# Channel shuffle on one core: tiles of 32 KB a partition in place of 24 KB, three buffers a side in place of four

## Chip, cores, metric

One core of a Trainium2 chip. The time is the device time of one execution in microseconds (us). A run of a kernel gives one such time; each kernel was run several times, and medians are quoted with lowest and highest. The profile is one recorded execution; its span, from the first to the last instruction, is about 1.8 us shorter than the time of the same execution. The TensorE clock granted was 1.0 of full speed in every run. A run more than 1.5% above the fastest of its kernel is called slow and left out of the comparisons; the others are called fast.

## The reference

```python
x = x.reshape(batch, h, w, groups, channels_per_group)   # 16, 64, 64, 8, 32, float32
x = x.transpose(0, 1, 2, 4, 3)
return x.reshape(batch, h, w, c)                         # 16, 64, 64, 256
```

No arithmetic: in each pixel's 256 channels an 8 x 32 table is transposed. 67.11 MB are read and 67.11 MB written.

## The kernel before

A tile takes 128 x q consecutive pixels. Each of the 128 partitions gets q pixels, which are q x 256 floats or q KB, one contiguous run in HBM, the memory outside the core; the distance between the starts of two partitions' runs, here also q KB, is called the row pitch. The load is issued from SP, the copy that permutes runs on VectorE (DVE in the profile), the store is issued from ACT. A tile pool of n buffers means that load i+n waits for copy i, and copy i+n for store i.

```python
_SIZES = [4, 8, 16] + [24] * 20 + [4]
_IN_BUFS = 4
_OUT_BUFS = 4
# ... pools in_pool and out_pool with these numbers of buffers, each of the biggest size
    for q in _SIZES:
        in_tile = in_pool.tile([P, biggest * c], F32, name="in_tile")
        nc.sync.dma_start(out=in_tile[:, : q * c], in_=rows(x_flat, first, q))
        out_tile = out_pool.tile([P, biggest * c], F32, name="out_tile")
        nc.vector.tensor_copy(
            out=out_tile[:, : q * c].rearrange("p (i j g) -> p i j g", j=CPG, g=G),
            in_=in_tile[:, : q * c].rearrange("p (i g j) -> p i j g", g=G, j=CPG),
        )
        nc.scalar.dma_start(out=rows(out_flat, first, q), in_=out_tile[:, : q * c])
        first += P * q
```

## Time and profile before

| | before |
|---|---|
| time | 317.05 us (316.96 to 317.16, 3 runs) |
| span of the profile | 315.3 us |
| VectorE busy | 122.0 us, 39% |
| moved | 134.22 MB, 426 GB/s over the span, 432 in the middle |
| load, issue to landing (median) | 52.3 us |
| store, issue to landing (median) | 31.2 us |

Most views of this profile are in the prediction. One more, the groups of instructions with shapes kept apart, is what the copies' costs were taken from. After the count come busy time in us and mean ns of one copy, then the idle time before these copies and what ended it.

```profile
L49 DVE COPY out_tile<-in_tile 128x6144 f32<-128x6144 f32 x20 | 113.9, 5694 | 169.2 <-DMA in_tile<-in_x_dram 169.2
L49 DVE COPY out_tile<-in_tile 128x4096 f32<-128x4096 f32 x1 | 3.9, 3881 | 3.9 <-DMA in_tile<-in_x_dram 3.9
L49 DVE COPY out_tile<-in_tile 128x2048 f32<-128x2048 f32 x1 | 2.0, 2024 | 1.4 <-DMA in_tile<-in_x_dram 1.4
```

VectorE idles longer than it works, and always until a load lands.

### The profile page before, as it was taken

How to read it: one execution, taken by the hardware profiler on the slowest of the kernel's cores; microseconds unless marked ns; L12 is line 12 of the kernel's file. 1: busy time of each engine (PE TensorE's matmuls, PEld its weight loads, DVE VectorE, ACT ScalarE, POOL GpSimd, SP SyncE). 2: the span in 40 equal slices, each digit the busy share in tenths (PEclk: the TensorE clock that was granted, in tenths of full speed). 3: DMA queues.
4: the chain of work that ended last, by engine and by line, in shares of the span. 5: the costliest groups of instructions: out<-in, count | busy, mean ns of one | idle time of the engine just before them, and what ended most of it. 6: DMA issues, size and time to landing. Idle time of an engine off the chain costs nothing.

```text
span 315.3 us, 178 instructions
## 1 busy us (share of the span) xinstructions
DVE 122.0 (39%) x24; POOL 0.2 (0%) x4
## 2 busy tenths in 40 slices
DVE  2525706243351707071533426170706244351710
POOL 0000000000000000000000000000000000000000
DMA  8999999999999999999999999999999999999997
GB/s 318 409 398 438 431 433 446 421 430 446 424 427 446 424 427 446 424 427 446 424 427 446 427 424 446 430 421 446 433 418 446 433 418 446 436 418 446 419 443 319
DMA packets 6912, 134.22 MB, mean 426 GB/s; under 512 B 768, under 2 KB 768, under 8 KB 1280
## 3 DMA queue, kind: packets, MB, share of 16 engines
q1 hardware_dynamic: 3456, 67.11, 49.9%
q10 hardware_dynamic: 3456, 67.11, 49.5%
HBM read 67.11 MB, written 67.11 MB: 426 GB/s over the span
## 4 chain that ended last, share of the span: by engine, by line
DMA 36%; another core or an unknown queue 33%; DVE 26%; SPq 0%; issue 0%; DVEq 0%
DMA in_tile<-in_x_dram 36%; DVE out_tile L49 26%; SPq L47 0%; DVEq L49 0%
## 5 line engine op out<-in xcount | busy, mean ns | idle before, releaser
L49 DVE COPY out_tile<-in_tile 128x6144 f32<-128x6144 f32 (+3 forms) x24 | 122.0, 5082 | 181.6 <-DMA in_tile<-in_x_dram 181.6
L71 POOL MEMSET const-bfloat16-1.0<- 128x1 bf16 x1 | 0.1, 101 | 0.0
L71 POOL MEMSET const-uint8-127<- 128x1 uint8 x1 | 0.1, 101 | 0.0
L71 POOL MEMSET const-float32-0.0<- 128x1 f32 x1 | 0.1, 98 | 0.2 <-issue 0.2
L71 POOL MEMSET const-float32-1.0<- 128x1 f32 x1 | 0.1, 98 | 0.0
## 6 DMA issues: line engine op xcount, KB each, us to landing
in_tile<-in_x_dram SPq DMA_DIRECT2D x20, 3072.0 KB, 52.3
out_dram<-out_tile ACTq DMA_DIRECT2D x20, 3072.0 KB, 31.2
in_tile<-in_x_dram SPq DMA_DIRECT2D x1, 2048.0 KB, 11.0
out_dram<-out_tile ACTq DMA_DIRECT2D x1, 2048.0 KB, 23.5
in_tile<-in_x_dram SPq DMA_DIRECT2D x2, 512.0 KB, 24.8
in_tile<-in_x_dram SPq DMA_DIRECT2D x1, 1024.0 KB, 5.5
out_dram<-out_tile ACTq DMA_DIRECT2D x2, 512.0 KB, 11.7
out_dram<-out_tile ACTq DMA_DIRECT2D x1, 1024.0 KB, 19.0
```

Of the source, the lines that this page charges most:

```text
L49: nc.vector.tensor_copy(out=out_tile[:, : q * c].rearrange("p (i j g) -> p i j g", j=CPG, g=G), in_=in_tile[:, : q * c].rearrange("p (i g ...
L71: nc = _bacc.Bacc("TRN2", target_bir_lowering=False, num_devices=1)
```

## The change

Its intent: fewer and larger transfers in the same memory. Per partition, 2 x 4 buffers of 24 KB and 2 x 3 buffers of 32 KB are both 192 KB. The small tiles at the ends stay.

```diff
-_SIZES = [4, 8, 16] + [24] * 20 + [4]
-_IN_BUFS = 4
-_OUT_BUFS = 4
+_SIZES = [4, 8, 16] + [32] * 15 + [4]
+_IN_BUFS = 3
+_OUT_BUFS = 3
```

## The prediction

> **What bounds the kernel now.** The kernel only moves data: every tile is loaded, its channels are permuted by one VectorE copy, and it is stored. I read the page first, for the engines and the totals:
>
> ```profile
> span 315.3 us, 178 instructions
> DVE 122.0 (39%) x24; POOL 0.2 (0%) x4
> DMA  8999999999999999999999999999999999999997
> GB/s 318 409 398 438 431 433 446 421 430 446 424 427 446 424 427 446 424 427 446 424 427 446 427 424 446 430 421 446 433 418 446 433 418 446 436 418 446 419 443 319
> DMA packets 6912, 134.22 MB, mean 426 GB/s; under 512 B 768, under 2 KB 768, under 8 KB 1280
> ```
>
> VectorE works 39% of the span. The DMA engines are full in every slice but the first and the last, and the rate repeats round 432 GB/s with no dip. The 134.22 MB are the input read once and the output written once, which the change cannot reduce. The packet line tells how tiles become packets: 24 tiles x 2 directions x (128 partition rows + 16 small ones) = 6912, and the small ones, 24 x 2 x 16 = 768, are those under 512 B. So one partition's row of a tile is one packet, of 24 KB now; I take the 16 small ones to be completion marks.
>
> Next the windows, cut at the starts of copies, to separate the steady stretch from the ends:
>
> ```profile
> 2.00:6.66 4.66, 1.10 (x2) 0.00 (x0) 1.00 1.02 412
> 6.66:12.61 5.95, 2.02 (x2) 0.00 (x0) 1.00 1.01 399
> 12.61:22.09 9.48, 3.88 (x2) 0.00 (x0) 1.00 1.01 418
> ...
> 46.66:293.90 247.24, 96.83 (x17) 0.00 (x0) 1.00 1.00 432
> 293.90:302.40 8.50, 5.68 (x1) 0.00 (x0) 1.00 1.02 438
> 302.40:313.30 10.90, 1.10 (x1) 0.00 (x0) 1.00 0.98 419
> ```
>
> The columns end with DMA share and GB/s. From 46.66 to 293.90 us seventeen copies start, one every 247.24 / 17 = 14.543 us. In that time a 24 KB tile goes in and another out: 2 x 128 x 24576 B = 6.291 MB, which makes 432.6 GB/s. At that rate all 134.22 MB would take 310.3 us; the span is 315.3. The other 5.0 us are the ends: 2.0 us before data flows, about 1.0 us because the stretch from 2.00 to 22.09 us moves 8.26 MB where 432.6 GB/s needs 19.1 us of its 20.1, and some 2 us at the end, while the last stores drain and the completions come back. The measured 317.05 us are 1.75 us more than the span.
>
> Last the waits, for what keeps the queues fed:
>
> ```profile
> DVE out_tile L49 <- DMA in_tile<-in_x_dram: 181.6, 24, 8.9
> SPq L47 <- DVE out_tile L49: 105.1, 20, 5.8
> in_tile<-in_x_dram SPq DMA_DIRECT2D x20, 3072.0 KB, 52.3
> out_dram<-out_tile ACTq DMA_DIRECT2D x20, 3072.0 KB, 31.2
> ```
>
> All 24 copies wait for their load, none for a store buffer. A load is issued when the copy four tiles earlier ends and lands when its own copy begins: 4 x 14.54 - 5.7 = 52.5 us, and the listing says 52.3. So three loads or more are always queued. A store lands 31.2 us after issue, two tile times. Both queues always hold work: the transfer rate is the bound, and VectorE's regular 8.8 us of idling is its consequence.
>
> **What the Trainium skill says.** (1) "DMA: Bandwidth & Descriptors", section "Where 436 GB/s comes from", puts a ceiling of 435.2 GB/s on the DMA side of SBUF. The trace agrees: 432.6 is 99.4% of it, leaving hardly anything for larger packets to win. (2) The same page, "Anatomy of one DMA — SWDGE (gpsimd) path", gives each DMA a fixed cost of about 2 us, mostly the wait for the last byte's receipt. These transfers are issued from SP and ACT, not that path, and the trace shows the cost hidden: two such DMAs end in each 14.543 us, while the bytes alone need 6.291 MB / 435.2 GB/s = 14.456 us. Only 0.087 us a tile is left for all overhead. (3) The same page, "Latency and other measured facts", has copies slowing when HBM row pitches are large powers of two: 207 GB/s a direction at 512 KiB against 214 at full rate, 164 at 2 MiB. Our pitch becomes 32 KiB, sixteen times below the first of these. The trace has one 16 KB-pitch tile and its rate says little, as it mixes with small stores. (4) "Perfetto Trace Analysis", "Identifying Performance Opportunities", reads repeated bubbles on the engine that should be saturated as a possible lack of buffers. The bubbles here are on VectorE, which should not be saturated; the DMA engines have none.
>
> **The change part by part.** *Bytes and buffers.* 28 + 20 x 24 + 4 = 512 KB a partition becomes 28 + 15 x 32 + 4 = 512. Buffers stay at 4 x 24 + 4 x 24 = 3 x 32 + 3 x 32 = 192 KB a partition. The byte time of 310.3 us stays.
>
> *Fewer transfers.* Twenty large loads and stores become fifteen; packets become 19 x 2 x 144 = 5472 if a 32 KB row stays one packet. If the 0.087 us a tile is all paid per packet or per DMA, five tiles fewer save 5 x 0.087 = 0.43 us; if it is proportional to bytes, nothing. I take 0.25 us. The new tile time is then between 14.543 x 4/3 = 19.39 and 14.456 x 4/3 + 0.087 = 19.36 us.
>
> *Copies.* By shape the listing gives 2024, 3881 and 5694 ns for 2048, 4096 and 6144 elements, so the last 2048 cost 1.81 us and a copy of 8192 takes about 7.5 us. Busy: 15 x 7.5 + 2 x 1.10 + 2.02 + 3.88 = 120.6 us (was 122.0). It lies beside the transfers, with 19.4 - 7.5 = 11.9 us idle before each. Worth 0.
>
> *Three load buffers.* Load i+3 is issued when copy i ends. Load i+1 has by then run 7.5 of its 19.4 us and i+2 is queued behind it, so the load queue holds (19.4 - 7.5) + 19.4 = 31 us of work at each refill. Landing time 3 x 19.4 - 7.5 = 50.6 us, near the old 52.3. At the start the first 32 KB load must now wait for copy 0, which ends at 5.25 us; the loads ahead of it are busy until 12.6 us. Worth 0.
>
> *Three store buffers.* This is the tighter place. Now a store is done 5.7 + 31.2 = 36.9 us after its tile landed, 2.54 tile times, where 4 = 58.2 us are allowed: 21 us spare. The lag arises at the start, where small store packets alternate with large load packets, so I expect it to keep its size counted in tiles. Then after the change a store is done 2.54 x 19.4 = 49.2 us after its tile landed, landing about 42 us after issue, where 3 x 19.4 = 58.2 us are allowed: 9 us spare. Worth 0. Even if a copy had to wait, the load queue's 31 us would have to run dry first.
>
> *The ends.* The opening 4, 8, 16 and the closing 4 KB tile are the same, so the 5.0 us stay. When the last large tile lands, its store comes 7.5 us later (was 5.7). The stores still queued then are 1.5 tiles (2.54 less the tile just landed), 30 us of work at half the rate or 15 us alone, so no hole opens.
>
> Sum: 317.05 - 0.25 + 0 + 0 + 0 = 316.8 us.
>
> **The rivals.** *A fixed cost per DMA that really is paid.* At the skill's 2 us, five transfers fewer in each queue, with the queues side by side, would save 10 us: 307 us, 3% faster. For it: the smaller tiles of the first 22 us do run slower. Against it: the 0.087 us above; a saving of 10 us would require about 447 GB/s over the steady part, above the ceiling, and the trace holds no slice-long average over 446. *Power-of-two rows.* Rows 32 KB apart may make engines that march together meet in one part of HBM. At the 3% that the skill gives for 512 KiB (207 against 214) on the 290 us of large tiles: 9 us more, 326 us. For it: 24 KB rows are no power of two, so before cannot show it. Against: the skill's smallest slow pitch is far larger, and here tiles lie contiguously. *Store buffers run out.* If the store lag exceeds three tiles, copies begin to wait for stores, VectorE's idle time is split between the two, and loads are issued later. With 31 us of loads queued I would give that 0 to 2 us: up to 319 us. For it: spare time falls from 21 to 9 us. Against: the lag in before is steady, with all large stores near the median of 31.2 (maximum 31.3).
>
> **Range and chances.** The sum of known effects spans 316.6 to 317.05. Widened by small losses at the ends and a milder form of the pitch or buffer rival, 315.8 to 318.4 should hold eight times in ten. Over 2% faster (under 310.7) needs the ceiling broken: 0.01. Over 2% slower (over 323.4) needs the pitch rival nearly whole: 0.04. Within 2%: 0.95.
>
> **What would show it.** Right: large copies 19.36 to 19.39 us apart, each about 7.5 us and waiting only for its load; some 432 to 434 GB/s in the middle slices; 5472 packets; loads landing in about 50.6 us, stores in about 42; the first and last slices as before. Wrong: a middle rate under 428 (pitch), copies that wait for stores (buffers), tile times clearly under 19.3 us (a per-DMA cost), more packets than 5472 (rows split), or a hole in the last 20 us.

## The result and the profile after

After: 316.84 us (316.67 to 316.93, 4 runs). Before, beside it: 317.06 us (316.96 to 317.16, 4 runs). The ratio is 0.9995, 95% interval 0.998 to 1.001: the same. (Here and below a ratio is the mean time of one kernel's fast runs over that of the other's of the same rounds, so not quite the ratio of the medians quoted.)

The head of the page after, with the lines that answer to those of before:

```profile
span 315.2 us, 150 instructions
...
DVE 119.9 (38%) x19; POOL 0.2 (0%) x4
...
DMA  8999999999999999999999999999999999999996
GB/s 314 408 422 458 403 449 408 457 408 453 412 453 412 458 412 453 420 445 428 437 428 437 437 428 437 428 437 433 437 433 437 428 441 424 445 420 426 439 441 291
DMA packets 5472, 134.22 MB, mean 426 GB/s; under 512 B 608, under 2 KB 608, under 8 KB 1120
```

The span, the mean rate and the full row of nines are those of before. The rate swings more from slice to slice in the first half (403 to 458), which no run explains; from 80 to 280 us both kernels move 433 GB/s. There are 5472 packets, as worked out: a 32 KB row is still one packet.

The copies by shape, then the two waits and the landing times of the large transfers:

```profile
L49 DVE COPY out_tile<-in_tile 128x8192 f32<-128x8192 f32 x15 | 111.9, 7459 | 166.2 <-DMA in_tile<-in_x_dram 166.2
```

```profile
DVE out_tile L49 <- DMA in_tile<-in_x_dram: 179.3, 19, 11.9
SPq L47 <- DVE out_tile L49: 105.1, 16, 7.6
```

```profile
in_tile<-in_x_dram SPq DMA_DIRECT2D x15, 4096.0 KB, 50.5
out_dram<-out_tile ACTq DMA_DIRECT2D x15, 4096.0 KB, 42.4
```

All 19 copies wait for their load and none for a store, as before. The load's landing time of 50.5 us is 3 x 19.37 - 7.5 = 50.6: a load is issued the moment a copy frees its buffer, and two more are queued ahead of it.

The windows after, cut at the starts of copies, with DMA share and GB/s last:

```profile
2.00:6.66 4.66, 1.11 (x1) 0.00 (x0) 1.00 1.03 417
6.66:12.74 6.08, 2.02 (x2) 0.00 (x0) 1.00 1.05 412
12.74:24.38 11.64, 3.83 (x2) 0.00 (x0) 1.00 1.02 432
...
74.22:287.23 213.01, 82.03 (x11) 0.00 (x0) 1.00 1.00 433
287.23:298.20 10.97, 7.47 (x2) 0.00 (x0) 1.00 1.01 435
298.20:313.20 15.00, 1.08 (x1) 0.00 (x0) 1.00 0.97 415
```

From 74.22 to 287.23 us eleven copies start, one every 213.01 / 11 = 19.365 us. With the 14.543 us of before this gives the two terms of a tile: 8.389 - 6.291 = 2.097 MB more take 19.365 - 14.543 = 4.822 us, so bytes go at 434.9 GB/s, and 14.543 - 6.291 MB / 434.9 GB/s = 0.077 us a tile is left for everything else. Twenty large tiles cost 20 x 14.543 = 290.9 us and fifteen 15 x 19.365 = 290.5. The steady part gave 0.4 us by this sum. The medians differ by 0.2 us, so the ends should have taken the other 0.2 back; but the interval above includes no difference at all, so neither figure is shown by the times.

### The profile page after: what moved, and what is told of

Same layout as the page of the kernel before. It is cut to its first block, busy times and chain, and to the rows that moved or that the text cites. A ratio compares the mean times of both kernels' runs of the same rounds, so it can differ in the third digit from the quotient of the medians.

```text
span 315.2 us, 150 instructions
## 1 busy us (share of the span) xinstructions
DVE 119.9 (38%) x19; POOL 0.2 (0%) x4
## 2 busy tenths in 40 slices
DMA packets 5472, 134.22 MB, mean 426 GB/s; under 512 B 608, under 2 KB 608, under 8 KB 1120
## 4 chain that ended last, share of the span: by engine, by line
DMA 40%; another core or an unknown queue 30%; DVE 25%; issue 0%; DVEq 0%; SPq 0%
DMA in_tile<-in_x_dram 40%; DVE out_tile L49 25%; DVEq L49 0%; SPq L47 0%
## 5 line engine op out<-in xcount | busy, mean ns | idle before, releaser
L49 DVE COPY out_tile<-in_tile 128x8192 f32<-128x8192 f32 (+3 forms) x19 | 119.9, 6313 | 179.3 <-DMA in_tile<-in_x_dram 179.3
## 6 DMA issues: line engine op xcount, KB each, us to landing
in_tile<-in_x_dram SPq DMA_DIRECT2D x15, 4096.0 KB, 50.5
out_dram<-out_tile ACTq DMA_DIRECT2D x15, 4096.0 KB, 42.4
in_tile<-in_x_dram SPq DMA_DIRECT2D x1, 2048.0 KB, 11.1
```

The costliest lines, as they stand in the source:

```text
L49: nc.vector.tensor_copy(out=out_tile[:, : q * c].rearrange("p (i j g) -> p i j g", j=CPG, g=G), in_=in_tile[:, : q * c].rearrange("p (i g ...
```

## The experiments

Theory: the transfer rate is the bound, tile size and buffers are spare, and a tile costs its bytes at 434.9 GB/s plus about 0.08 us. Rivals: three buffers hurt and large tiles hid it; large tiles gain and the power-of-two row pitch takes it back; a fixed cost per transfer is really paid; VectorE or the small tiles at the ends are on the path. All kernels gave the correct result. They came in three batches, on different chips, each beside its own runs of the kernel before: 316.94, 316.96 and 316.99 us. The ratios below are to these. The kernel after was not run again beside them.

### Three buffers, old tiles

```diff
-_SIZES = [4, 8, 16] + [32] * 15 + [4]
+_SIZES = [4, 8, 16] + [24] * 20 + [4]    # 3 load and 3 store buffers kept
```

> Half of the change alone: 24 KB tiles as before, but three load and three store buffers. Theory (the transfer rate binds, buffers are spare): 317.0 us, within 0.3 of the kernel before; tiles 14.54 us apart; loads landing in about 3 x 14.54 - 5.7 = 37.9 us, stores in 31.2, no copy waiting for a store (done 36.9 us after the tile landed, 43.6 allowed). Rival (three buffers are too few and the change's larger tiles hid that): 319 us or more, with copies that wait for stores.

Measured: 317.00 us (316.91 to 317.03), ratio 1.0001 (0.9988 to 1.0013). Loads landed in 37.8 us, stores in 30.5, all 24 copies waited for loads. The fourth pair of buffers was worth nothing; three buffers of either size are enough.

### Rows of 30 KB

```diff
-_SIZES = [4, 8, 16] + [32] * 15 + [4]
+_SIZES = [4, 8, 16] + [30] * 16 + [4]
```

> Sixteen tiles of 30 KB, a row pitch that is no power of two, with three buffers each. Theory (a tile costs its bytes at 434.9 GB/s plus 0.077 us, from the tile times 14.543 and 19.365 us of the two kernels): tiles 7.864 MB / 434.9 GB/s + 0.077 = 18.16 us apart, 316.8 to 316.9 us in all. Rival (a gain from fewer transfers was given back to the power-of-two pitch of 32 KB): tiles clearly under 18.1 us apart and under 315.5 us in all.

Measured: 316.52 us (316.50 to 316.63), ratio 0.9987 (0.9975 to 1.000). Copies 70.92 to 288.81 us are 217.89 / 12 = 18.16 us apart, the theory's figure. So no gain was hidden behind the 32 KB pitch. The time is 0.3 us below the forecast, at the ends since the middle is as forecast, and is the lowest of all kernels here, but its interval reaches 1.

### Tiles of 8 KB

```diff
-_SIZES = [4, 8, 16] + [32] * 15 + [4]
-_IN_BUFS = 3
-_OUT_BUFS = 3
+_SIZES = [4] + [8] * 63 + [4]
+_IN_BUFS = 12
+_OUT_BUFS = 12
```

> 63 tiles of 8 KB between two of 4, with twelve buffers each, so the same memory. It takes the cost per tile times 65 in place of 19. Theory (0.077 us a tile): tiles 2.097 MB / 434.9 GB/s + 0.077 = 4.90 us apart, and 46 x 0.077 = 3.5 us more than after in all, about 320 us. Rival (about 2 us per transfer really paid, in each queue): 46 x 2 = 92 us more, about 409 us. A cost of 0.5 us would show as 340 us.

Measured: 321.47 us (321.45 to 322.05), ratio 1.0148 (1.0132 to 1.0164). That is 4.6 us more than after for 46 more tiles, 0.10 us a tile where 0.077 were expected. The fixed cost is real, but for a load and a store together it is a twentieth of 2 us. This is with further transfers always queued; no run has the cost without them. Whether it is paid by the DMA or by its packets is not separated, as each tile has the same number of both.

### Two buffers a side

```diff
-_IN_BUFS = 3
-_OUT_BUFS = 3
+_IN_BUFS = 2
+_OUT_BUFS = 2
```

> The kernel after with two load and two store buffers. A store needs 49.2 us from the landing of its tile and only 2 x 19.37 = 38.7 are now allowed, so copies must wait for stores. Theory (a copy's wait costs only if both DMA queues run dry, and at any moment a store is queued): 317 to 318.5 us, the waits of the copies now split between loads and stores. Rival (waits for store buffers are paid in full): 10 us at each of some 13 tiles, over 400 us; paid in part: over 323 us.

Measured: 318.24 us (317.90 to 319.11), ratio 1.0044 (1.0031 to 1.0058). The list of waits turned over, while the middle kept its rate:

```profile
DVE out_tile L49 <- DMA out_dram<-out_tile: 180.6, 17, 12.3
DVE out_tile L49 <- DMA in_tile<-in_x_dram: 5.3, 2, 3.9
```

```profile
62.00:280.00 218.00, 87.44 (x12) 0.00 (x0) 1.00 1.00 433
```

Seventeen copies now wait for a store buffer, 180.6 us in all, and it costs 1.3 us against the kernel before, outside the middle. The lesson is in these two fences together: VectorE's waits changed their releaser, and the rate in the middle did not change. I had expected the waits to be split between loads and stores. They are all put down to the stores, because a load and the store before it now finish almost together and the store is last.

### Each copy twice

```diff
-        nc.vector.tensor_copy(...)
+        for _ in range(2):
+            nc.vector.tensor_copy(...)       # the same copy
```

> The kernel after with every copy done twice (same result). VectorE works 240 of 317 us. Theory (copies lie beside transfers): a store is done 49.2 + 7.5 = 56.7 us after its tile landed at most, 58.1 allowed; 316.8 to 317.4 us, large copies in pairs of 15 us, tiles still 19.37 us apart. Rival (the copy is on the path, by its end or by the issue of loads): 15 x 7.5 = 112 us more if in full, 7.5 us more (324) if only the last copy is exposed.

Measured: 317.13 us (316.94 to 318.71, 6 runs), ratio 1.0016 (1.0001 to 1.0031); five of the six lie within 316.94 to 317.90. VectorE worked 241.8 us of a 316.6 us span in the profiled run, the one at 318.71. In that run tiles were 19.50 us apart, not the 19.37 expected; the runs nearer the median have no profile. 120 us of added work cost about 0.2 us in the median: the copy is beside the transfers.

### The last tile a large one

```diff
-_SIZES = [4, 8, 16] + [32] * 15 + [4]
+_SIZES = [4, 8, 16, 4] + [32] * 15
```

> The kernel after with the closing 4 KB tile moved to the start, so that the last tile is one of 32 KB. Theory (30 us of stores at half rate, or 15 us alone, are queued when the last tile lands, so its copy of 7.5 us is covered): 316.6 to 317.2 us. Rival (the small last tile shortens the exit): the exit grows by 7.5 - 1.1 = 6.4 us, 323 us.

Measured: 316.91 us (316.81 to 316.96), ratio 0.9998 (0.9986 to 1.001). The last copy, of 7.5 us, is covered by stores still queued. The small closing tile is worth nothing.

### No small tiles

```diff
-_SIZES = [4, 8, 16] + [32] * 15 + [4]
+_SIZES = [32] * 16
```

> Sixteen equal tiles of 32 KB, no small tile at either end, three buffers each. Theory (time is bytes over rate plus about 2 us at each end; a full queue of loads keeps the engines busy until stores come): the rate is 433 GB/s from about 2 us on, the 1.0 us that small tiles cost at the start is won back, 315.6 to 316.2 us; store lag only about two tile times, as large rows now alternate with large ones from the start. At the end the store of the last tile comes 7.5 us after its landing and the stores queued then last about as long, so up to 1 us may be lost. Rival (the small tiles fill the pipeline early and that is worth what they bring forward): the first store starts 14 us later than in the kernel after and the time is up to 14 us longer, 325 to 331 us.

Measured: 324.30 us (323.67 to 324.92), ratio 1.0231 (1.0218 to 1.0245): 2.3% slower, where my theory expected a small gain. The rival named about the right size, but for a reason that the profile refutes: it put the loss into a late start. The time is lost in the middle. Here is the timeline of this kernel's copies (start, duration, shape, idle before and its releaser):

```profile
41.33 7.50 DVE L49 COPY out_tile<-in_tile 128x8192 f32<-128x8192 f32 x1 [11.26 <-DMA in_tile<-in_x_dram]
61.36 7.50 DVE L49 COPY out_tile<-in_tile 128x8192 f32<-128x8192 f32 x1 [12.52 <-DMA in_tile<-in_x_dram]
81.51 7.61 DVE L49 COPY out_tile<-in_tile 128x8192 f32<-128x8192 f32 x1 [12.65 <-DMA in_tile<-in_x_dram]
...
300.64 7.57 DVE L49 COPY out_tile<-in_tile 128x8192 f32<-128x8192 f32 x1 [11.88 <-DMA in_tile<-in_x_dram]
```

Copies are (300.64 - 61.36) / 12 = 19.94 us apart, 3% more than the 19.365 of the kernel after, with the same tiles, buffers and waits. The stretch from 80 to 280 us moved 424 GB/s, where the kernel after moved 433 (columns as in the windows above; then the stores' landing time):

```profile
80.00:280.00 200.00, 75.36 (x10) 0.00 (x0) 1.00 1.00 424
out_dram<-out_tile ACTq DMA_DIRECT2D x16, 4096.0 KB, 34.4
```

The trace's packet records say which packets: from 80 to 280 us a 32 KB load packet took 1259 ns in the mean and the slowest hundredth over 1950, a store packet 1215; in the kernel after both take 1213. So the loads are what slows, and only some of them: 13.9% of the load packets took over 5% longer than usual, and none in the kernel after.

### No small tiles at the start only

```diff
-_SIZES = [4, 8, 16] + [32] * 15 + [4]
+_SIZES = [32] * 15 + [24, 8]
```

> Fifteen tiles of 32 KB, then 24 and 8; no ramp at the start. Theory: as sixteen equal tiles, but the last store is asked for 2 us after its landing instead of 7.5, so no hole can open at the end: 315.4 to 316.0 us, the fastest so far by about 0.3%. Rival (early small tiles matter): 325 to 331 us.

Measured: 324.09 us (323.70 to 324.61), ratio 1.0228. The same loss and again 424 GB/s in the middle, so the end is not its place. What the missing small tiles do to the middle, 40 us and more after they would have been done, was open. One clue is the offset between the two streams. With sixteen equal tiles the first store is issued at 20.4 us, two us before the second load has landed (its copy starts at 22.6), so the first store and the third load set out almost together, and from then on a store follows a load through the tiles at a short distance. The last batch varied that.

### A first tile of 4 KB

```diff
-_SIZES = [32] * 16
+_SIZES = [4, 28] + [32] * 15
```

> Sixteen equal tiles were 7 us slower, against the theory, and their middle ran at 424 GB/s in place of 433. Here the first of them is split in 4 and 28, so all later tiles have the same addresses as there. Theory P (the middle is slow because stores walk through their rows nearly in step with the loads, a store finishing 2 to 4 us after a load; a small first tile starts stores while the next load is under way and sets another offset): the middle is back at 433 GB/s, tiles 19.37 us apart, 316.0 to 316.8 us. Theory A (the 4 MB alignment of the addresses slows the middle): 323 to 325 us.

Measured: 317.04 us (316.95 to 317.13), ratio 1.0001. The middle is back at 433 GB/s with copies 19.37 us apart: the addresses of the tiles are not the cause by themselves. The total shows no gain over the kernel after, where 0 to 0.8 us were expected; fewer small tiles bought nothing.

### Rows of 30 KB, no small tiles at the start

```diff
-_SIZES = [32] * 16
+_SIZES = [30] * 17 + [2]
```

> Seventeen tiles of 30 KB and one of 2, no ramp: the stores start in step with the third load as with sixteen equal tiles, but no row or tile lies a power of two from the next. Theory P alone (being in step is enough): the middle is 2 to 3% slow, 321 to 325 us. Theory P with the power of two (both are needed): tiles 18.16 us apart, 315.8 to 316.6 us.

Measured: 317.76, 318.61 and 321.20 us, one run at 324.35 left out as slow, though its clock is that of the others and it may be the very loss sought here; ratio 1.0068 (1.0017 to 1.0119). Neither forecast holds cleanly. The profiled run, at 317.76, had 433 GB/s and 18.22 us a tile in the middle. The spread of the fast runs is 1%, against 0.12% for the kernel before in this batch. This does not settle whether the power of two matters.

### Tiles in another order

```diff
-_SIZES = [32] * 16; tiles in order
+    for n in range(16):
+        first = (5 * n % 16) * P * 32
```

> Sixteen equal tiles of 32 KB taken in steps of five (0, 5, 10, 15, 4 ...), so that the tile stored lies 10 tiles, or 6 the other way, from the tile loaded, in place of 2; in time all is as with sixteen equal tiles. If the interference is between addresses in HBM whose distance counts beyond 4 MB: the middle changes, to 433 GB/s and 316 us or to something slower still. If only the position within a tile counts, in HBM or in SBUF: as sixteen equal tiles, 323.5 to 325 us.

Measured: 324.17 us (323.81 to 325.89), ratio 1.0236, 424 GB/s in the middle. As with sixteen equal tiles in order, so in these two orders the distance in whole tiles between the stored and the loaded address did not matter.

### No small tiles, each copy twice

```diff
 _SIZES = [32] * 16
-        nc.vector.tensor_copy(...)
+        for _ in range(2):
+            nc.vector.tensor_copy(...)       # the same copy
```

> Sixteen equal tiles of 32 KB with each copy done twice, so the first store starts 7.5 us later, when the third load has some two packets of each engine to go: same addresses, same tiles, another offset in time. Theory P: stores are out of step, the middle runs at 431 to 433 GB/s, and although VectorE does twice the work the kernel is faster than sixteen equal tiles with one copy: 316 to 319 us, the end included. Theory A or any cost of a late first store: 324 us or more, 331 if the 7.5 us are added.

Measured: 316.94 us (316.79 to 317.08), ratio 0.9997 (0.9982 to 1.0012). Doing the copy twice makes this kernel 7.4 us faster than doing it once. The page's rate row shows where:

```profile
GB/s 333 399 466 399 399 462 404 458 408 441 424 433 433 433 433 433 433 433 433 433 433 433 433 433 433 433 433 433 433 433 433 433 437 433 433 437 429 441 429 325
```

The middle is a flat 433 GB/s, and no load packet from 80 to 280 us took over 5% longer than usual:

```profile
80.00:280.00 200.00, 155.34 (x22) 0.00 (x0) 1.00 1.00 434
out_dram<-out_tile ACTq DMA_DIRECT2D x16, 4096.0 KB, 42.3
```

Addresses, tiles and buffers are those of sixteen equal tiles. What moved is when transfers are asked for: each store, and each load that waits for a buffer, follows a landed tile by 15 us of copies in place of 7.5. VectorE's added work is not needed for the full rate, as the first tile of 4 KB reached it with single copies. That also clears the late first store: here it starts later still, at 28.0 us against 20.4.

### The offsets put together

How far behind a load a store lands follows from the profile: copy time plus the store's landing time, less whole tile times (a minus sign: just before one). These are medians; in the slow kernels the tile times and landings wander by a us or two. The first column is the kernel; one row of 32 KB in and one out take an engine 19.37 / 8 = 2.4 us.

| kernel | copy + store landing, us | tile time, us | store behind a load, us | middle |
|---|---|---|---|---|
| after | 7.5 + 42.4 | 19.37 | 11.1 | full |
| last tile large | 7.5 + 41.4 | 19.37 | 10.2 | full |
| copies twice (the run at 318.71 us) | 15.1 + 37.0 | 19.50 | 13.1 | 0.7% slow |
| two buffers | 7.5 + 31.1 | 19.37 | -0.1 | full |
| first tile of 4 KB | 7.5 + 31.3 | 19.37 | 0.1 | full |
| no small tiles, copies twice | 15.0 + 42.3 | 19.40 | -0.9 | full |
| no small tiles | 7.5 + 34.4 | 19.94 | 2.0 | 3% slow |
| other order | 7.5 + 34.6 | 19.97 | 2.2 | 3% slow |
| no small tiles at the start | 7.5 + 36.0 | 19.96 | 3.6 | 3% slow |
| 30 KB, none at the start | 7.1 + 33.3 | 18.22 | 3.9 | full in the profiled run, times scattered |

Three kernels not in the table fit in at the full rate: 7.8 us in the kernel before, 7.1 with three buffers and 24 KB, 9.9 with 30 KB and all small tiles. The tiles of 8 KB are left out, as their cost per tile lowers the rate by itself.

The three kernels that lose 3% are those with 32 KB rows whose stores follow the loads by 2 to 4 us, about one to one and a half rows of an engine. My theory P named that distance, from two slow kernels already seen, and holds for the third, but its wording, that being nearly in step is slow, fell: closer still (-0.1 and 0.1 us) is fast. The share of load packets that took over 5% longer than usual from 80 to 280 us sorts the kernels in the same way: 13.4 to 13.9% in these three, 0.9% in the copies done twice, at most 0.1% in all others.

That the timing of the transfers is the cause is shown by the kernel of equal tiles with copies done twice: the same transfers from the same addresses, asked for at other times. That the distance between store and load is what counts in that timing fits the table and is not shown: the three slow kernels all start alike, so they are nearly one point, and the copies done twice lost 0.7% at 13.1 us. Where the two streams get in each other's way, in HBM or in SBUF, why it is the loads that stretch, and whether the 32 KB pitch is needed, stays open.

No experiment points to a version that clearly beats both kernels. Ten of the fourteen kernels, before and after among them, have medians of their fast runs between 316.5 and 318.6 us; the 16 x 30 KB version is lowest, 0.13% below before with an interval that reaches 1.

## Why the prediction was right, point by point

- **Bytes at a fixed rate: right.** 432.6 GB/s before, 433.2 after (8.389 MB / 19.365 us). The ceiling of 435.2 GB/s in the Trainium skill ("DMA: Bandwidth & Descriptors", section "Where 436 GB/s comes from") was not passed over the middle of any kernel (434 at most). One argument was weak: slices up to 446 already lie above that ceiling, so that no slice passed 446 said nothing about it.
- **Fewer transfers, 0.25 us: the tile time right, the total within the noise.** The tile time was given as 19.36 to 19.39 us and is 19.365. The steady part gained 0.4 us, the upper end of 0 to 0.43; the medians moved 0.2 us, which the noise does not separate from nothing. That this is so near 0.25 is luck: 0.25 was a choice within the range. The tiles of 8 KB put the cost per tile at 0.10 us, a little over the bound of 0.087 that was worked out from the ceiling.
- **Copies, worth 0: right.** 7.46 us against 7.5; VectorE busy 119.9 us against 120.6. Doubling them cost about 0.2 us.
- **Three load buffers, worth 0: right.** Landing time 50.5 us against 50.6. With the old tiles three buffers changed nothing either.
- **Three store buffers, worth 0: right, and the margin too.** A store is done 7.5 + 42.4 = 49.9 us after its tile landed, against 49.2 forecast and 58.1 allowed. That the lag keeps its size in tiles held here (2.54 before, 2.58 after), and that it comes from the small first tiles fits: without them it is 41.9 / 19.94 = 2.10. How they make it was not tested. Taking the margin away with two buffers cost 1.3 us, inside the 0 to 2 us given for that rival.
- **The ends stay: right within the noise.** By the sum above they took back about 0.2 us. The claim that no hole opens was tested by making the last tile large: no loss.
- **The rival of the power-of-two rows: rightly set aside for this kernel, but the prediction asked only about the pitch.** At the offset of 11 us that the small first tiles leave, 32 KB rows run at full rate. At 2 to 4 us they lose 3%, the size that I had put to this rival; whether the pitch has a part in that loss was not settled. The prediction did not consider the timing between loads and stores at all. In this it was lucky: the change kept the small first tiles (the "ramp" of the texts above), and without those at the start the same 32 KB tiles are 2.3% slower.

## What to carry to other kernels

When the transfer rate in the middle is flat and at its ceiling, work out what a tile costs beyond its bytes from two tile sizes before making tiles larger: here it was 0.08 us (0.10 by the smallest tiles), so that regrouping twenty large tiles could win about 2 us at most by this sum. A compute engine that waits is no sign of a loss while both DMA queues hold work: here its waits changed from loads to stores for 1.3 us, and its work doubled for 0.2 us. But the timing of loads and stores alone made the difference between 424 and 433 GB/s here, so measure the middle rate again whenever the first tiles change, even if every wait looks the same.

## What the Trainium skill lacked or had wrong

- "DMA: Bandwidth & Descriptors", section "Where 436 GB/s comes from", says that for transfers between HBM and SBUF the HBM side (about 358 GB/s) binds. Here one core moved 433 GB/s in the middle, loads and stores together, within 0.5% of the fabric figure of the same section (435); that page's own measurement of one core alone, 425, is above 358 too. "HBM Reference", section "Specifications (TRN2)", is nearer with about 425 for a core that streams alone.
- "DMA: Bandwidth & Descriptors", section "Anatomy of one DMA — SWDGE (gpsimd) path", gives about 2 us fixed for a DMA; it has no figure for what is left of it when transfers of the SP and ACT queues are always queued: 0.08 to 0.10 us a tile, a load and a store together.
- No page that I read has the effect of the offset between a load and a store stream: with 32 KB rows, 424 GB/s where stores land 2.0 to 3.6 us behind loads, 433 to 434 at -0.9 to 0.1 us and at 10 to 11 us; the same transfers took 324.3 us at 2.0 us and 316.9 at -0.9. That the offset is what counts is not shown, only that the timing does.
- "DMA: Bandwidth & Descriptors", section "Latency and other measured facts", measures slow copies from a row pitch of 512 KiB. Pitches of 24, 30 and 32 KB, laid out contiguously, all ran at 433 GB/s at a good offset; the page says nothing of copies that lose 3% at 32 KB at a bad one.
